# A decoder trunk on one core: three weight buffers made 64 bytes longer each, so that the operands behind them begin at other places of 512 bytes

## The chip, the cores and the metric

The kernel runs on one core of a Trainium2 chip. The metric is the device time of one execution in microseconds (us). All inputs and the output lie in the chip's main memory (HBM); the core works on a memory of 128 partitions (SBUF) and the matrix engine writes its sums to a small accumulator memory (PSUM).

## The reference

One layer of a decoder trunk on 2048 tokens of width 1024, in float32:

```python
mod = (c_act @ w_ada[l] + b_ada[l])[:, None, :]
sh1, sc1, g1, sh2, sc2, g2 = jnp.split(mod, 6, axis=-1)
h = rms_norm(x) * (1.0 + sc1) + sh1
x = x + g1 * token_mixer(h, w_in[l], ..., pos)
h = rms_norm(x) * (1.0 + sc2) + sh2
x = x + g2 * conv_ffn(h, w_up[l], conv_w[l], conv_b[l], w_down[l])
return rms_norm(x) * final_gain
```

`token_mixer` is one input projection, three groups of causal recurrent heads (retention, HGRN2, GLA) and one output projection. `conv_ffn` is an up-projection to 2 x 2816 columns, a causal convolution of width 3, a gated product and a down-projection.

## The kernel before

**Matrix products in halves.** Every large float32 product is made of three matmuls of the type float32r. Each operand is split into a high part (`hi`, the value rounded by a copy on ScalarE) and a low part (`lo`, the rest, by a subtraction on VectorE), and `split3` (L241 to L243) adds hi x hi, hi x lo and lo x hi into one accumulator. A matmul has one operand that is loaded into the matrix engine ahead of it (LDWEIGHTS, 128 columns; PEld in the profile) and one that is streamed through it (512 or 256 columns). The load of the next matmul runs beside the stream of the present one.

**The mixer** (four blocks of 512 tokens) takes about the first half of the time. `piece` (L217) and `tf512` (L281) fetch a piece of a weight matrix of 128 x 1024 values into a raw buffer and split it into `hi` and `lo`; `cf_gemm`, `tf_gemm` and `tf512` multiply the pieces with the normed input `h` (tile `ha`, both parts), `unit_g` multiplies `h` with a narrow weight of 32 columns (`alow`, L729 and L730), and `out_half` multiplies the mixer's outputs `oT` with `wout`. Between them lie the small float32 matmuls of the recurrences (`lvh`, `uh`, `ur` and others).

**The gated MLP** (two halves of 1024 tokens) follows. Up and down projections use a scheme with seven products in place of eight for a 2 x 2 block product; their operands are the tiles `A` and `dA` (weights, from `w4_tile`, L962) and `B` and `dB` (inputs, from `hc_tile`, L953).

**Order.** The order on the matrix engine is written out by hand (a clock in the program decides where the small matmuls go between the large ones); the other engines are ordered by a scheduler from the same program. All DMAs but 56 are issued from SP's queue.

**Where buffers lie.** Pools take room in the order in which they are opened: constants, `h`, `a4`, `w`, `tmp`, `x`, and then the mixer's `unit` and `const1`, whose room `gemm` takes over for the MLP. The pool `w` holds, in this order, two raw buffers (`wraw`), three high parts (`whi`) and three low parts (`wlo`), each 4096 bytes per partition. In the MLP the same eight buffers serve in turn as places for `A` and `dA`. All of this stands in the allocation of the built program, from which the following places are taken; "place" means the start address within a partition, modulo 512 bytes. Before the change every float32r operand begins at place 128, the slices of `alow` excepted, which are 128 bytes wide and begin at 128, 256, 384 and 0 in turn.

Of the kernel before, what the change touches and what calls it, by code (L numbers as in the profile page):

```python
# [10 lines left out]
F32R = mybir.dt.float32r  # L11
# [6 lines left out]
P = 128  # L18
# [36 lines left out]
class Clock:  # L55
# [15 lines left out]
    def adv(self, us):  # L71
        self.t += us
        while self.due and self.due[0][0] <= self.t:
            self._next()
# [26 lines left out]
def trunk(ctx, tc, xT, vecs, cvec, cst, rope, msk, wada, win, walow, wgla, wout, wup, wdown, out):  # L101
# [6 lines left out]
    pw = sb("w", 3)  # L108
# [9 lines left out]
    def acc_ps(name):  # L118
        return pp.tile([P, 512], F32, tag="acc", name=name, bufs=4)
# [17 lines left out]

    V, S, G, T = nc.vector, nc.scalar, nc.gpsimd, nc.tensor

    vec = pc.tile([P, 117], F32, tag="vec", name="vec")  # L140
    nc.sync.dma_start(vec[:], vecs[:, 0:117])
    c_all = pc.tile([P, NC_], F32, tag="cst", name="c_all")
# [62 lines left out]
    def keep(key, t):  # L205

        kept[key] = pdr.tile([P, 1024], F32, tag=f"kept{key}", name=f"kept{key}")
        nc.sync.dma_start(kept[key][:], t.bitcast(F32))
# [3 lines left out]
    def ada_next():  # L212
        m = later.pop(0) if later else None
        if m is not None:
            ada(m)

    def piece(src, name, key, both=False, ahead=50):  # L217

        ada_next()
        with tc.high_priority(offset=ahead):  # L220
            hi = pw.tile([P, 1024], F32R, tag="whi", name="h" + name)
            lo = pw.tile([P, 1024], F32R, tag="wlo", name="l" + name)
            if key + "h" in kept:
                nc.sync.dma_start(hi[:].bitcast(F32), kept[key + "h"][:])
                nc.sync.dma_start(lo[:].bitcast(F32), kept[key + "l"][:])
                return hi, lo
            raw = pw.tile([P, 1024], F32, tag="wraw", name="r" + name, bufs=NRAW)
            nc.sync.dma_start(raw[:], src)
            S.copy(hi[:], raw[:])
            if key + "l" in kept:  # L230
                nc.sync.dma_start(lo[:].bitcast(F32), kept[key + "l"][:])
            else:
                V.tensor_tensor(lo[:], raw[:], hi[:], op=ALU.subtract)  # L233
                if both:
                    keep(key + "h", hi[:])
                keep(key + "l", lo[:])
        return hi, lo

    def split3(ps, lhs, rhs, first, last, more=False):

        T.matmul(ps, lhs[0], rhs[0], start=first, stop=False, skip_group_check=more)  # L241
        T.matmul(ps, lhs[0], rhs[1], start=False, stop=False, skip_group_check=more)  # L242
        T.matmul(ps, lhs[1], rhs[0], start=False, stop=last, skip_group_check=more)  # L243

    h = [None] * KD
# [5 lines left out]
    def cf_gemm(name, i, parts=(slice(0, TB),)):  # L251
        if name in ready:
            return ready.pop(name)
        hi, lo = piece(win[i], name, f"i{i}")
        ps = acc_ps("ps" + name)
        for ts in parts:
            for k in range(KD):
                sl = slice(k * P, (k + 1) * P)
                split3(ps[:, ts], (hi[:, sl], lo[:, sl]), (h[k][:, 0, ts], h[k][:, 1, ts]), k == 0, k == KD - 1)
                adv(3 * M512)  # L260
        return ps
# [19 lines left out]
    def tf512(name, i):  # L281

        pss = [acc_ps(f"ps{name}_{c}") for c in range(NCH)]
        for q4 in range(4):
            half, sub = q4 // 2, q4 % 2
            src = win[i + half:i + half + 3:2][:, :, sub * 512:(sub + 1) * 512].rearrange("a p n -> p a n")
            ada_next()
            with tc.high_priority(offset=50):
                raw = pw.tile([P, 2, 512], F32, tag="wraw", name=f"r{name}_{q4}", bufs=NRAW)
                nc.sync.dma_start(raw[:], src)  # L290
                hi = pw.tile([P, 2, 512], F32R, tag="whi", name=f"h{name}_{q4}")
                lo = pw.tile([P, 2, 512], F32R, tag="wlo", name=f"l{name}_{q4}")
                S.copy(hi[:], raw[:])
                key = f"t{i}_{q4}l"
                flat = lo[:].rearrange("p a n -> p (a n)")
                if key in kept:
                    nc.sync.dma_start(flat.bitcast(F32), kept[key][:])
                else:
                    V.tensor_tensor(lo[:], raw[:], hi[:], op=ALU.subtract)
                    keep(key, flat)  # L300
            for c in range(NCH):
                cs = slice(c * P, (c + 1) * P)
                for kk in range(2):
                    k = half * 4 + sub * 2 + kk
                    sl = slice(kk * 256, (kk + 1) * 256)
                    split3(pss[c][:].rearrange("p (a n) -> p a n", a=2), (h[k][:, 0, cs], h[k][:, 1, cs]),
                           (hi[:, :, sl], lo[:, :, sl]), k == 0, k == KD - 1)
                    adv(3 * M512)
        return pss
# [60 lines left out]
    def startup():  # L370
# [8 lines left out]
        def weight(name, i, extra=False):  # L379
            raw = pw.tile([P, 1024], F32, tag="wraw", name="r" + name, bufs=NRAW)  # L380
            nc.sync.dma_start(raw[:], win[i])
            if extra:
                t = [pa.tile([P, 1024], F32R, tag="a4k", name=n + name) for n in "hl"]
            else:
                t = [pw.tile([P, 1024], F32R, tag="w" + n, name=n[0] + name) for n in ("hi", "lo")]
            W[name] = [*t, raw, i]

        def cast(name):
# [9 lines left out]
        def load(*ms):  # L398
            for m in ms:
                raws[m] = ada_load(m, True)  # L400
        load(8, 0)
        weight("f", 1)
        load(9)
        weight("q", 0)
        load(1, 2)
        acc = new_acc("n1_0")
# [47 lines left out]
        for k, (ld, first, then, wl) in enumerate(plan):  # L454
            if k == 0:
                weight("v0", 2)
            if k == 3:
                weight("v1", 3, True)
            load(*ld)
            for m in first:  # L460
                cond(m)
            scaled(x[k], bc[:], k)
            high(x[k], k, "0_")
            if k in (1, 4):
                name = "v0" if k == 1 else "v1"
                cast(name)
                parts[0].add(name)
            for m in then:
                cond(m)
            low(x[k], k)  # L470
            if wl:
                low_part(wl)
                parts[1].add(wl)
            pending += [(kind, k, w) for w in (0, 1) for kind in "fqv"]
            flush()
# [413 lines left out]
    def out_piece(b, half, i):  # L889
        return piece(wout[half * 4 + i], f"wo{b}_{half}_{i}", f"o{half * 4 + i}",  # L890
                     both=True, ahead=250 if (b, half) == (0, 0) else 600 if (b, half) == (NB - 1, 1) else 50)
# [57 lines left out]
    def take(ring, places):  # L949
        nth[ring] += 1  # L950
        return places[(nth[ring] - 1) % len(places)]
# [9 lines left out]

    def w4_tile(name):  # L962
        tag, bufs = take("w4", W4)
        return pw.tile([P, 1024], F32R, tag=tag, name=name, bufs=bufs)

    R_H, R_HC, R_A4 = [(ph, "h", 8, True)] * 8, [(None, "hc", 8, True)] * 8, [(pa, "a4k", NA4, True)] * NA4
# [20 lines left out]
    def up_op(A, s, f, i, src):  # L987
        t = w4_tile(f"A{s}_{f}_{i}")
        A[i] = split(src, t[:, 0:512], t[:, 512:1024])
# [307 lines left out]
    def last_operands(s):  # L1297

        r = []
        for k in range(NF // 2):  # L1300
            nm = f"{s}_3_{k}"
            with tc.high_priority(offset=60):
                ra = raw_half(sums["d", k][:, BLOCK[3], :], "rd" + nm)
                at = pa.tile([P, 1024], F32R, tag="a4k", name="dA" + nm) if k < 8 else w4_tile("dA" + nm)
                A = split(ra, at[:, 0:512], at[:, 512:1024])
                rb = t2k("rb" + nm)
                nc.sync.dma_start(rb[:], gs[s, 3, k][:])
                bt = ph.tile([P, 2, 512], F32R, tag="h", name="dB" + nm, bufs=8) if k < 8 else \
                    pg.tile([P, 2, 512], F32R, tag="hc", name="dB" + nm, bufs=8)
                r.append((A, split(rb[:], bt[:, 0, :], bt[:, 1, :])))  # L1310
        return r
# [233 lines left out]
def _build(arrays):  # L1545
    import concourse.bacc as bacc
    nc = bacc.Bacc("TRN2", target_bir_lowering=False, num_devices=1)
    aps = [nc.dram_tensor(n, a.shape, mybir.dt.from_np(a.dtype), kind="ExternalInput").ap()
           for n, a in arrays.items()]
    out = nc.dram_tensor("out", (NB, P, KD, TB), F32, kind="ExternalOutput").ap()  # L1550
    with tile.TileContext(nc) as tc:
        trunk(tc, *aps, out)
    return nc
# [10 lines left out]
```

## Time and profile before

| | us |
|---|---|
| median of three timed runs | 2562.22 |
| lowest and highest of them | 2557.1 and 2563.71 |
| span of the profiled execution | 2557.2 |
| PE (matmuls) busy in it | 2493.1 |
| PEld (weight loads) busy | 2132.7 |
| DVE busy | 1973.8 |
| ACT busy | 1139.0 |

The profiled execution is one of its own; the page gives its span from the first to the last instruction and no further time for it. The span lies at the low end of the three timed runs, 5.0 us (0.2%) under their median. PE is the matrix engine, DVE is VectorE, ACT is ScalarE. A matmul's end is modelled in the profile: a matmul of 512 columns is shown with 0.39 us, though the next one starts earlier. The pace is therefore read from the starts.

### The profile page before, as it was taken

What the parts mean: (1) busy time and instruction counts of PE and PEld (TensorE: products, weight loads), DVE (VectorE), ACT (ScalarE), POOL (GpSimd) and SP (SyncE); (2) the same over time, 40 slices, a digit from 0 to 9 for tenths busy, and PEclk for the clock granted to TensorE, in tenths of its full rate; (3) what the DMA queues carried; (4) which work ended last, traced back from release to release, by engine and by line L of the source; (5) the groups of instructions that cost most, each with busy time, mean ns of one, the idle gap of its engine ahead of it and who ended that gap; (6) DMA issues with size and microseconds to landing.
All of it is one profiled execution on the core that took longest, in us unless ns stands there. A gap on an engine that the chain in (4) does not pass through costs nothing.

```text
span 2557.2 us, 37116 instructions
## 1 busy us (share of the span) xinstructions
PE 2493.1 (97%) x13146; PEld 2132.7 (83%) x13146; DVE 1973.8 (77%) x3596; ACT 1139.0 (45%) x1914; POOL 169.6 (7%) x303
## 2 busy tenths in 40 slices
PE   5999999999999999999899999999999999999998
PEld 4898888988889898898788888888878888888887
DVE  8788986878678776787688888887677778778666
ACT  4433434524444235333254555455444555455442
POOL 1000000000000000000200000000001001000000
PEclk9999999999999999999999999999999999999999
DMA  8454576775687847786745444477675544447663
GB/s 304 166 190 165 197 250 214 250 251 196 220 309 278 291 147 242 267 308 223 278 168 174 153 146 163 149 274 244 210 228 168 155 146 145 154 136 251 221 193 127
DMA packets 229337, 533.84 MB, mean 209 GB/s; under 512 B 25216, under 2 KB 28320, under 8 KB 229152
## 3 DMA queue, kind: packets, MB, share of 16 engines
q1 hardware_dynamic: 224672, 516.80, 59.5%
q0 software_dynamic: 4480, 14.68, 1.6%
q8 instruction: 103, 1.69, 0.3%
q14 instruction: 82, 0.67, 0.1%
HBM read 397.69 MB, written 133.69 MB: 208 GB/s over the span
## 4 chain that ended last, share of the span: by engine, by line
PE 78%; issue 9%; DVE 5%; DMA 4%; ACT 1%; SPq 0%; POOL 0%; DVEq 0%; ACTq 0%; POOLq 0%
PE X L241 6%; PE X L242 6%; PE X L243 6%; PE Z L241 3%; PE Z L242 3%; PE Z L243 3%; PE lvh L610 3%; PE y L241 2%; PE y L243 2%; PE y L242 2%; PE psqkvgr L243 2%; PE psqkvgr L241 2%; PE psqkvgr L242 2%; PE psvgh L242 2%; PE psvgh L241 2%
## 5 line engine op out<-in xcount | busy, mean ns | idle before, releaser
L241 PE MATMUL X<-B,A 128*128 128x512 f32 x572 | 223.5, 391 | 1.4 <-ACT u L1247 1.4
L242 PE MATMUL X<-B,A 128*128 128x512 f32 x572 | 222.9, 390 | 0.0
L243 PE MATMUL X<-B,A 128*128 128x512 f32 x572 | 222.9, 390 | 0.0
L974 DVE TENSOR_TENSOR dA<-rd,dA 128x512 fp32r<-128x512 f32 x154 | 106.1, 690 | 86.7 <-ACT dA L973 86.4
L973 ACT CAST dA<-rd 128x512 fp32r<-128x512 f32 x154 | 95.6, 621 | 139.9 <-PE dX L243 45.8
L974 DVE TENSOR_TENSOR A<-s,A 128x512 fp32r<-128x512 f32 x176 | 120.8, 686 | 43.7 <-ACT A L973 43.3
L973 ACT CAST A<-s 128x512 fp32r<-128x512 f32 x176 | 108.7, 618 | 71.5 <-PE Z L243 45.2
L241 PE MATMUL psvgh<-hvgh,ha 128*128 128x256 f32 x480 | 140.0, 292 | 0.0
L241 PE MATMUL dX<-dB,dA 128*128 128x512 f32 x352 | 137.1, 390 | 0.0
L243 PE MATMUL dX<-dB,dA 128*128 128x512 f32 x352 | 137.1, 390 | 0.0
L242 PE MATMUL dX<-dB,dA 128*128 128x512 f32 x352 | 137.1, 390 | 0.0
L242 PE MATMUL psvgh<-lvgh,ha 128*128 128x256 f32 x480 | 135.9, 283 | 1.1 <-DVE lvgh L233 1.1
L243 PE MATMUL psvgh<-hvgh,ha 128*128 128x256 f32 x480 | 135.9, 283 | 0.0
L241 PEld LDWEIGHTS X<-B,A 128*128 128x128 f32 x572 | 107.5, 188 | 24.3 <-ACT u L1247 2.2
L243 PEld LDWEIGHTS X<-B,A 128*128 128x128 f32 x572 | 107.5, 188 | 22.1
L242 PEld LDWEIGHTS X<-B,A 128*128 128x128 f32 x572 | 107.5, 188 | 22.1
L610 PEld LDWEIGHTS lvh<-qbh,kh 128*128 128x128 f32 x896 | 115.2, 191 | 8.8 <-issue 1.0
L610 PE MATMUL lvh<-qbh,kh 128*128 128x128 f32 x896 | 120.1, 277 | 1.1 <-DVE kh L620 1.0
L241 PE MATMUL Z<-B,A 128*128 128x512 f32 x308 | 120.6, 392 | 0.0
L242 PE MATMUL Z<-B,A 128*128 128x512 f32 x308 | 120.5, 391 | 0.0
L243 PE MATMUL Z<-B,A 128*128 128x512 f32 x308 | 120.4, 391 | 0.0
L974 DVE TENSOR_TENSOR dB<-rb,dB 128x512 fp32r<-128x512 f32 x154 | 105.7, 687 | 13.2 <-ACT dB L973 13.1
(463 smaller groups left out, 7129.8 us busy)
## 6 DMA issues: line engine op xcount, KB each, us to landing
gs<-yv SPq DMA_DIRECT2D x154, 256.0 KB, 2.8
rb<-gs SPq DMA_DIRECT2D x154, 256.0 KB, 4.0
r<-wup SPq DMA_DIRECT2D x141, 256.0 KB, 3.3
s<-sumsu SPq DMA_DIRECT2D x132, 256.0 KB, 3.0
wada<-wada SPq DMA_DIRECT2D x48, 512.0 KB, 5.1
rd<-sumsd SPq DMA_DIRECT2D x88, 256.0 KB, 3.8
rd<-wdown SPq DMA_DIRECT2D x66, 256.0 KB, 3.8
x<-xT SPq DMA_DIRECT2D x64, 256.0 KB, 5.6
```

Of the source, the lines that this page charges most:

```text
L241: T.matmul(ps, lhs[0], rhs[0], start=first, stop=False, skip_group_check=more)
L242: T.matmul(ps, lhs[0], rhs[1], start=False, stop=False, skip_group_check=more)
L243: T.matmul(ps, lhs[1], rhs[0], start=False, stop=last, skip_group_check=more)
L610: T.matmul(ps[:, c * P:(c + 1) * P].rearrange("p (h n s) -> p h n s", h=2, s=s), kq[:, c * P:(c + 1) * P], rhs, start=True, stop=True)
L973: S.copy(hi, src)
L974: V.tensor_tensor(lo, src, hi, op=ALU.subtract)
```

## The change

Each `whi` buffer is allocated with 1040 columns of 4 bytes in place of 1024, and the first 1024 are used. The four places that made such a tile now call one helper.

```diff
+    def high_part(name):
+
+        return pw.tile([P, 1024 + 16], F32R, tag="whi", name=name)[:, 0:1024]
+
@@ piece
-            hi = pw.tile([P, 1024], F32R, tag="whi", name="h" + name)
+            hi = high_part("h" + name)
@@ tf512
-                hi = pw.tile([P, 2, 512], F32R, tag="whi", name=f"h{name}_{q4}")
+                hi = high_part(f"h{name}_{q4}").rearrange("p (a n) -> p a n", a=2)
@@ weight (startup)
-                t = [pw.tile([P, 1024], F32R, tag="w" + n, name=n[0] + name) for n in ("hi", "lo")]
+                t = [high_part("h" + name), pw.tile([P, 1024], F32R, tag="wlo", name="l" + name)]
@@ w4_tile
+        if tag == "whi":
+            return high_part(name)
```

In the built program this moves the second `whi` buffer by 64 bytes, the third by 128, and everything that lies behind them (`wlo`, and the pools `tmp`, `x`, `unit`, `const1`, `gemm`) by 192. Constants, `h`, `a4`, the raw buffers and the first `whi` buffer stay.

| place of 512 | before | after |
|---|---|---|
| `h`, `a4`, `wraw`, first `whi` | 128 | 128 |
| second, third `whi` | 128 | 192, 256 |
| `wlo`, `te`, `xy`, `hc`, most of `unit` | 128 | 320 |
| `kT`, `o`, `kk` (small float32 matmuls) | 320 | 0 |

## The prediction

> **What bounds the kernel now.** I read the page's totals first, then four stretches of the MLP.
>
> ```profile
> span 2557.2 us, 37116 instructions
> PE 2493.1 (97%) x13146; PEld 2132.7 (83%) x13146; DVE 1973.8 (77%) x3596; ACT 1139.0 (45%) x1914; POOL 169.6 (7%) x303
> ...
> 1400.00:1500.00 100.00, 100.00 (x443) 82.85 (x442) 83.31 (x106) 49.30 (x74) 7.01 (x20) 1.00 0.48 156
> 1700.00:1800.00 100.00, 100.00 (x443) 82.88 (x442) 69.94 (x110) 51.08 (x89) 0.00 (x0) 1.00 0.80 269
> 2000.00:2100.00 100.00, 100.00 (x443) 82.92 (x442) 78.28 (x97) 50.33 (x75) 9.54 (x11) 1.00 0.50 154
> 2200.00:2300.00 100.00, 100.00 (x443) 82.91 (x442) 77.60 (x95) 51.29 (x74) 9.35 (x10) 1.00 0.44 140
> ```
>
> PE is shown busy for 97% of the span. That alone says little, since a matmul's end is modelled. The stretches say more: their columns are the stretch, its length, busy time and count of PE, PEld, DVE, ACT and POOL, the granted clock, the DMA share and GB/s. In each 100 us exactly 443 matmuls are under way, at full clock, whether DMA is 0.44 or 0.80 busy and whether DVE is at 70 or at 83 us. So nothing but PE's own pace sets the time there. The timeline gives the pace; the first two rows are the first and the last of 28 matmuls of 512 columns that follow each other without a gap, the other two the first and the last of 15 of 256 columns:
>
> ```profile
> 1999.76 0.39 PE L242 MATMUL X<-B,A 128*128 128x512 f32 x1
> ...
> 2005.88 0.39 PE L242 MATMUL X<-B,A 128*128 128x512 f32 x1
> ```
> ```profile
> 517.18 0.28 PE L243 MATMUL psvgh<-hvgh,ha 128*128 128x256 f32 x1
> ...
> 518.85 0.28 PE L242 MATMUL psvgh<-lvgh,ha 128*128 128x256 f32 x1
> ```
>
> That is (2005.88 - 1999.76) / 27 = 226.7 ns for 512 columns and (518.85 - 517.18) / 14 = 119.3 ns for 256. The difference, 107.4 ns, is what 256 columns cost, so 512 columns cost 214.8 ns, and about **11.9 ns of each matmul do not depend on its width**. By the built program there are 8,422 float32r matmuls of 512 columns and 1,668 of 256: 8,422 x 0.2267 + 1,668 x 0.1193 = 2,108 us of the span. In these, the 11.9 ns amount to 10,090 x 0.0119 = 120 us. This is the only large sum on which the place of an operand could act.
>
> **The change, part by part.** The two built programs have the same 22,589 instructions in the same order on every engine, with the same waits; only addresses differ (and the row length of 1040 in the operands that lie in `whi`). So nothing is added, removed or moved in time by itself, and no queue sees another order. What remains are four possible prices.
>
> *1. PE reads with the two operands at other places.* A weight load runs beside the stream of the matmul before it. Before, the load and the stream beside it begin at the same place of 512 bytes in all cases but the 48 loads of `alow` at its other three places. After, by the built program, they begin at different places in 5,669 of the 8,422 and 1,184 of the 1,667 cases: about 6,850. What a different place costs or saves isn't shown for a full load. The nearest rows are those of `alow`, a narrower load with the same stream: its slices begin at 128, 256, 384 and 0 in turn, while the stream always begins at 128. Each place is used by two matmuls (L729, L730):
>
> ```profile
> 375.13 0.39 PE L729 MATMUL alg<-ha,alow 128*32 128x512 f32 x1
> 375.36 0.40 PE L730 MATMUL alg<-ha,alow 128*32 128x512 f32 x1
> 375.59 0.40 PE L729 MATMUL alg<-ha,alow 128*32 128x512 f32 x1
> 375.83 0.39 PE L730 MATMUL alg<-ha,alow 128*32 128x512 f32 x1
> 376.06 0.40 PE L729 MATMUL alg<-ha,alow 128*32 128x512 f32 x1
> 376.29 0.39 PE L730 MATMUL alg<-ha,alow 128*32 128x512 f32 x1
> 376.52 0.40 PE L729 MATMUL alg<-ha,alow 128*32 128x512 f32 x1
> 376.75 0.40 PE L730 MATMUL alg<-ha,alow 128*32 128x512 f32 x1
> 376.99 0.40 PE L241 MATMUL psakg<-ha,hakg 128*128 128x512 f32 x1
> ```
>
> The pair at the same place as the stream takes 375.59 - 375.13 = 0.46 us, the pairs that are 128, 256 and 384 bytes off take 0.47, 0.46 and 0.47. So none of the three other places saves the fixed 11.9 ns per matmul, and none adds it. The resolution: three pairs at other places take 376.99 - 375.59 = 1.40 us, 0.467 each, against 0.46; that is at most 3.3 ns per matmul. The second row of evidence is the small float32 matmuls, from the chain of work, eight of 128 columns in each group:
>
> ```profile
> 203.19 0.89 PE lvh L610 x8
> ...
> 211.10 0.89 PE uh L646 x8
> ...
> 297.63 0.89 PE ur L816 x8
> ```
>
> `lvh` reads both operands at place 128; `uh` and `ur` load `kT` and `kk` from 320 and stream `v` from 128. All take 0.89 us. They stream at a slower pace (0.89 / 8 = 111 ns for 128 columns), so they are the weaker evidence.
>
> There is also a reason from the rows why a start place should matter little:
>
> ```profile
> L729 PEld LDWEIGHTS alg<-ha,alow x32: 107/108/113, 59.1 to 983.5; 128*32 128x32 f32 x32
> ...
> L241 PEld LDWEIGHTS X<-B,A 128*128 128x128 f32 x572 | 107.5, 188 | 24.3 <-ACT u L1247 2.2
> ```
>
> A load of 32 columns is shown with 108 ns (the middle of the three figures), one of 128 with 188 (the mean), so a loaded column takes (188 - 108) / 96 = 0.83 ns, and a streamed one 107.4 / 256 = 0.42 ns. While the load goes through its 512 bytes, the stream goes through 1,024: their distance changes by 512 bytes and takes every value modulo 512 once, wherever they began. The start place moves that meeting, it doesn't take it away. I take **0** for this part, and keep 6,850 x 3.3 ns = 23 us to both sides as its bound, below nothing too.
>
> *2. DVE and ACT with operands at other places.* DVE's subtractions and products of 512 columns already come with all sorts of distances:
>
> ```profile
> L974 DVE TENSOR_TENSOR A<-s,A 128x512 fp32r<-128x512 f32 x176 | 120.8, 686 | 43.7 <-ACT A L973 43.3
> L700 DVE TENSOR_TENSOR qkh<-sqh,kh 128x512 f32<-128x512 f32 x16 | 11.0, 688 | 0.1
> L546 DVE TENSOR_TENSOR oh<-oh,sgh 128x512 f32<-128x512 f32 x16 | 11.0, 690 | 0.1
> L973 ACT CAST A<-s 128x512 fp32r<-128x512 f32 x176 | 108.7, 618 | 71.5 <-PE Z L243 45.2 <-DMA s<-sumsu 18.6 <-DVE s L1173 7.6
> L973 ACT CAST dB<-rb 128x512 fp32r<-128x512 f32 x154 | 94.9, 617 | 20.4 <-DMA rb<-gs 19.0 <-PE X L243 0.5
> ```
>
> `s` lies at place 224 and `A` at 128; `sqh`, `kh` and `qkh` all lie at 128; `oh` lies at 320 and `sgh` at 128. They take 686, 688 and 690 ns. ACT's casts take 618 and 617 ns, both from 224 to 128. I take 0. What covers a small loss is PE: of 100 us, DVE is busy 70 to 83 and ACT about 50.
>
> *3. DMA into and out of rows that begin elsewhere.* Every tile behind `whi` is moved by 192 bytes. How much DMA can matter is bounded by where PE waits for it, and by the start, the one stretch in which PE stands idle for long:
>
> ```profile
> PE y L243 <- DMA lwo<-kepto7l: 1.6, 1, 1.6
> PE y L241 <- DMA hwo<-kepto7h: 0.8, 1, 0.8
> ...
> 0.00:60.00 60.00, 33.09 (x164) 26.78 (x165) 47.94 (x83) 23.32 (x34) 12.06 (x24) 1.00 0.82 304
> ```
>
> PE's waits put down to DMA are 1.6 + 0.8 = 2.4 us in all; at the start 60 - 33.1 = 26.9 us are idle, in part for loads. If every load became 5% slower or faster (a guess, no row shows such a change), that would be 0.05 x (2.4 + 26.9) = 1.5 us. I take 0. The Trainium skill (DMA: Bandwidth & Descriptors, How a descriptor splits into AXI transactions) says that a row that doesn't begin at a multiple of 256 bytes costs extra beats; a row of 2,048 bytes would go from 68 beats at place 128 to 66 at place 320, an estimate of 3% less, which would make 0.9 us of those 29.3. No run here shows it.
>
> *4. Room.* The 192 bytes more change no pool's number of buffers, so no wait is made.
>
> The sum is 0 + 0 + 0 + 0, so a profiled execution would again span 2557.2 us. The median of the three runs stands 5.0 us above that, and the forecast is for such a median: **2562.2 us**.
>
> **The rivals.** *A: the 11.9 ns are a collision of the load with the stream beside it, and other places remove it.* It speaks for it that the amount is the same for 512 and 256 columns, as it would be if each load took something from the stream once, and that before the change every full load begins at the stream's place. Against it speak the `alow` pairs and the sweep. If it goes in all 6,850 cases, 6,850 x 0.0119 = 82 us go and the time is **2481 us**; at the bound of the `alow` rows it is 23 us, 2539. The Trainium skill (TensorE: Matmul & The Clock Gate, Part 1, "Wait — 56ns, not 53.3ns?") gives 215.7 ns between the starts of back-to-back matmuls of 512 columns, where the trace has 226.7; by it something does hold these up by 11 ns. Its figure is for bf16 matmuls, so it doesn't say what.
>
> *B: the same place is the good case, and other places cost.* When load and stream begin at the same place, they meet only at the ends of the load; from different places the stream overtakes the load in its middle. If that holds the stream up for two to three loaded columns (2.5 ns at 0.83 each), 6,850 x 2.5 ns = 17 us are added: **2579 us**; the bound above gives 2585. For it speaks that the `alow` pairs at other places are, if anything, the slower ones (0.467 against 0.46); against it that 0.01 us is one step of the view. It decides from 7.7 us / 6,850 = 1.1 ns per case on, since about 0.3% or 7.7 us is what a measurement here can tell from no change.
>
> *C: DMA sets something after all*, in the start or at the change from mixer to MLP, by up to 2 us to either side: 2560 to 2564. It can't be told from the forecast.
>
> That the change doesn't do what it says is excluded: the built program has the operands of the large matmuls at 128, 192, 256 and 320, and those of the small ones at 0 besides.
>
> **How the numbers follow.** The forecast has 0.62, A 0.18, B 0.16, C 0.04. C is within 0.3% for the most part; 0.01 of it goes to each side. So faster by over 0.3% gets 0.18 + 0.01 = 0.19, slower 0.16 + 0.01 = 0.17, and the rest, 0.64, is within 0.3%. The range takes in the bound of part 1 to both sides, 2562.2 - 23 and 2562.2 + 23: 2539 to 2585. It leaves out the full form of A and a little of B, some 0.14.
>
> **What would show it.** In the profile after: again 443 matmuls in each 100 us of the MLP, 27 steps of float32r matmuls in 6.12 us, `alow` pairs of 0.46 to 0.47 us though `alow` has moved to place 320, and DVE and ACT at 686 to 690 and 617 to 618 ns. A is right if the steps of matmuls with different places fall toward 215 ns while those with equal places (an `A` in the first `whi` with its `B` in an `h` tile) stay at 226.7. B is right if they rise by more than 1 ns. Equal steps and another time would mean that the waits at the start or between the stages have changed, and that part 3 is wrong.

## The result, and the profile after

The changed kernel takes 2584.3 us (median of 4 runs, 2581.43 to 2588.4) against 2562.97 us before (4 runs). The ratio is **1.0096, 95% interval 1.0084 to 1.0109**: about 24.6 us slower. That is 0.0096 of the time before, and the table below is in such microseconds; the two medians by themselves lie 21.3 us apart. The profiled execution took 2581.43 us, with a span of 2579.7, 22.5 us more than the span before. The forecast was no change, with a range of 2539 to 2585.

The totals of the page after, and the same four stretches of the MLP (stretch, length, then busy time and count of PE, PEld, DVE, ACT and POOL, granted clock, DMA share, GB/s):

```profile
span 2579.7 us, 37116 instructions
PE 2516.3 (98%) x13146; PEld 2128.2 (83%) x13146; DVE 1974.9 (77%) x3596; ACT 1136.1 (44%) x1914; POOL 170.1 (7%) x303
```
```profile
1400.00:1500.00 100.00, 100.00 (x437) 81.74 (x437) 83.53 (x106) 49.59 (x74) 7.70 (x22) 1.00 0.45 151
1700.00:1800.00 100.00, 100.00 (x436) 81.50 (x435) 72.94 (x111) 52.62 (x91) 0.00 (x0) 1.00 0.81 274
2000.00:2100.00 100.00, 100.00 (x435) 81.28 (x434) 75.91 (x92) 48.70 (x72) 9.37 (x10) 1.00 0.49 153
2200.00:2300.00 100.00, 100.00 (x435) 81.42 (x434) 78.20 (x96) 48.77 (x74) 9.48 (x11) 1.00 0.45 145
```

PE is still never idle there and the clock is still full, but only 435 to 437 matmuls are under way in 100 us in place of 443. That is 1.66%; on the 1,267 us from 1290 to the end it would make 21 of the 22.5 us. The starts of the first matmul of the up-projection and of the last `dX` of the down-projection, before and after, bear it out:

```profile
1227.36 0.58 PE L241 MATMUL X<-B,A 128*128 128x512 f32 x1
...
2510.28 0.39 PE L243 MATMUL dX<-dB,dA 128*128 128x512 f32 x1
```
```profile
1228.33 0.58 PE L245 MATMUL X<-B,A 128*128 128x512 f32 x1
...
2532.48 0.40 PE L247 MATMUL dX<-dB,dA 128*128 128x512 f32 x1
```

The MLP begins 1.0 us later and, up to that last `dX`, takes 22.2 - 1.0 = 21.2 us more. PE's busy time has grown by 23.2 us, and those of DVE, ACT and POOL have changed by 3 us at most. In the lines of the groups (busy us, mean ns of one), DVE and ACT take what they took; PE's waits for DMA sum to 2.2 us in place of 2.4; and the float32 matmuls, now with `kT` at place 0 and `vh` at 320, still take 0.89 us for eight:

```profile
L980 DVE TENSOR_TENSOR A<-s,A 128x512 fp32r<-128x512 f32 x176 | 120.7, 686 | 48.5 <-ACT A L979 48.1
L704 DVE TENSOR_TENSOR qkh<-sqh,kh 128x512 f32<-128x512 f32 x16 | 11.0, 686 | 0.1
L550 DVE TENSOR_TENSOR oh<-oh,sgh 128x512 f32<-128x512 f32 x16 | 11.0, 689 | 0.1
L979 ACT CAST dB<-rb 128x512 fp32r<-128x512 f32 x154 | 95.0, 617 | 20.2 <-DMA rb<-gs 18.8 <-PE X L247 0.5
```
```profile
PE y L247 <- DMA lwo<-kepto7l: 1.6, 1, 1.6
PE y L245 <- DMA hwo<-kepto7h: 0.6, 1, 0.6
```
```profile
240.69 0.89 PE lvh L614 x8
...
251.89 0.89 PE uh L650 x8
```

So what has changed is the pace of the float32r matmuls. The changed kernel has its own control, since its operands lie at several places. The timeline, put beside the built program's addresses, has long stretches in which load and stream keep one distance modulo 512 (place of the loaded operand less that of the streamed one beside it). First and last matmul of three of them:

```profile
2422.15 0.39 PE L245 MATMUL dX<-dB,dA 128*128 128x512 f32 x1
...
2430.10 0.39 PE L247 MATMUL dX<-dB,dA 128*128 128x512 f32 x1
```
```profile
1321.81 0.40 PE L245 MATMUL X<-B,A 128*128 128x512 f32 x1
...
1329.60 0.39 PE L246 MATMUL Z<-B,A 128*128 128x512 f32 x1
```
```profile
1751.50 0.40 PE L245 MATMUL dY<-dB,dA 128*128 128x512 f32 x1
...
1759.67 0.39 PE L247 MATMUL dX<-dB,dA 128*128 128x512 f32 x1
```

The first has distance 0 (both at 320): 7.95 us / 35 steps = 227.1 ns. The second has distance 192 (128 streamed, 320 loaded): 7.79 / 34 = 229.1. The third has 320 (320 streamed, 128 loaded): 8.17 / 35 = **233.4**. The same kernel, the same engines beside it, three paces. The single steps repeat: in the second stretch they run 226, 229, 232 ns over and over, in the third they alternate between 231 and 236.

### The profile page after: what moved, and what is told of

It is laid out like the page before. It is cut to its first block, busy times and chain, and to the rows that moved or that the text cites. A ratio compares the mean times of both kernels' runs of the same rounds, so it can differ in the third digit from the quotient of the medians.

```text
span 2579.7 us, 37116 instructions
## 1 busy us (share of the span) xinstructions
PE 2516.3 (98%) x13146; PEld 2128.2 (83%) x13146; DVE 1974.9 (77%) x3596; ACT 1136.1 (44%) x1914; POOL 170.1 (7%) x303
## 4 chain that ended last, share of the span: by engine, by line
PE 81%; issue 9%; DVE 4%; DMA 3%; ACT 1%; POOL 0%; SPq 0%; DVEq 0%; ACTq 0%; POOLq 0%
PE X L245 6%; PE X L247 6%; PE X L246 6%; PE lvh L614 3%; PE Z L245 3%; PE Z L247 3%; PE Z L246 3%; PE psvgh L246 2%; PE psvgh L245 2%; PE psvgh L247 2%; PE psqkvgr L246 2%; PE psqkvgr L245 2%; PE psqkvgr L247 2%; PE lvg L614 2%; PE y L245 2%
## 5 line engine op out<-in xcount | busy, mean ns | idle before, releaser
L980 DVE TENSOR_TENSOR A<-r,A 128x512 fp32r<-128x512 f32 x130 | 89.2, 687 | 33.0 <-ACT A L979 33.0
```

The source lines that it names most:

```text
L980: V.tensor_tensor(lo, src, hi, op=ALU.subtract)
```

## The experiments

The theory to be tested: only the distance between a load and the stream beside it sets the pace. Rivals: the place of each operand by itself (multiples of 128 bytes being good), the other engines' or DMA's work at moved rows, or which of the moved buffers are in it.

**Matmuls alone, a map of the distance.** Nothing of the trunk is computed; 48 matmuls in a row for each pair of places.

```python
def r32(o, q, n, cols=P):
    return lambda r: (st[:, o + (r % 8) * P:o + (r % 8) * P + cols],
                      mv[:, q + (r % 4) * 512:q + (r % 4) * 512 + n])
...
for o in range(0, 128, 4):
    run("S", 4 * o, r32(o, 0, 512), 512)
```

> This kernel leaves out the whole computation and runs matmuls alone, 48 in a row for each pair of places, with nothing beside them: S moves the loaded operand by 0 to 496 bytes in steps of 16, M the streamed one, B both, H is S with 256 columns, N with 32 loaded columns, F in float32, L is bf16, T has the third load of each three moved. Theory one (only the distance between load and stream modulo 512 counts): S at 0 and all of B at 226 to 228 ns per matmul; S at 64, 128, 320 and 384 at 231 to 234 and at 192 and 448 at 229 to 231, as in the changed kernel's MLP; M mirrors S (distance -d); H falls by 1 to 2 ns at 320 and 448; N and F stay flat within 2 ns. Rival one (the place of each operand by itself counts, 128-byte multiples being good): B rises at 64, 192, 320 and 448 and stays at 0, 128, 256, 384, and S is flat at 128, 256 and 384. Rival two (the places matter only beside other engines' work): all of S, M and B are flat at 226 to 228.

In the timeline each group of 48 is one row: start, length, name, count. The three letters behind the capital are the bytes, a for 0 to j for 9 (`Sage` is 064). A step is the difference of two starts divided by 48.

```profile
22.27 11.04 PE L55 MATMUL Saaa<-mv,st 128*128 128x512 f32 x48
33.15 11.05 PE L55 MATMUL Sabg<-mv,st 128*128 128x512 f32 x48
...
66.42 11.36 PE L55 MATMUL Sage<-mv,st 128*128 128x512 f32 x48
77.62 11.29 PE L55 MATMUL Saia<-mv,st 128*128 128x512 f32 x48
...
155.81 11.15 PE L55 MATMUL Sbjc<-mv,st 128*128 128x512 f32 x48
166.80 11.36 PE L55 MATMUL Scai<-mv,st 128*128 128x512 f32 x48
...
200.09 11.04 PE L55 MATMUL Scfg<-mv,st 128*128 128x512 f32 x48
210.97 11.05 PE L55 MATMUL Schc<-mv,st 128*128 128x512 f32 x48
...
477.32 11.08 PE L55 MATMUL Bage<-mv,st 128*128 128x512 f32 x48
488.24 11.08 PE L55 MATMUL Bbci<-mv,st 128*128 128x512 f32 x48
...
655.81 11.28 PE L55 MATMUL Nage<-mv,st 128*32 128x512 f32 x48
666.93 11.23 PE L55 MATMUL Nbci<-mv,st 128*32 128x512 f32 x48
...
744.27 10.88 PE L55 MATMUL Fage<-mf,sf 128*128 128x128 f32 x96
754.99 10.88 PE L55 MATMUL Fbci<-mf,sf 128*128 128x128 f32 x96
...
819.31 10.52 PE L55 MATMUL Laaa<-mh,sh 128*128 128x512 bf16 x47
829.48 11.28 PE L55 MATMUL Taaa<-mv,st 128*128 128x512 f32 x48
840.60 11.25 PE L55 MATMUL Tage<-mv,st 128*128 128x512 f32 x48
851.69 11.28 PE L55 MATMUL Tbci<-mv,st 128*128 128x512 f32 x48
...
873.89 11.04 PE L55 MATMUL Tcfg<-mv,st 128*128 128x512 f32 x48
884.77 11.25 PE L55 MATMUL Tdca<-mv,st 128*128 128x512 f32 x48
```

- Distance 0: (33.15 - 22.27) / 48 = 226.7 ns. 64: 11.20 / 48 = 233.3. 192: 10.99 / 48 = 229.0. **256: 10.88 / 48 = 226.7**, as good as 0. The whole curve from 256 to 496 repeats that from 0 to 240 within 0.2 ns, one step of the rows. So the distance counts modulo 256, not 512 as the theory had it; the theory's other numbers hold.
- Both operands moved together (B, 64 bytes): 10.92 / 48 = 227.5, nearly all of it in the first few matmuls. The place by itself doesn't count: rival one falls. Nothing ran beside these matmuls, and the paces differ all the same: rival two falls.
- 32 loaded columns (N, 64): 11.12 / 48 = 231.7, the same at all distances within 1.1 ns. float32 (F): 10.72 / 96 = 111.7 at all distances. Neither kind feels it.
- The streamed operand moved (M) mirrors S: 64 bytes give 229.2, 192 give 233.3. With only each third load 64 bytes off (T): 11.09 / 48 = 231.0, well over a third of the way from 226.7, which T has at 256 bytes (10.88 / 48). T's row at 0 looks slower only because the first start in it is recorded too early, 417 ns before the second; its later steps take 226.7. So the matmuls at the good distance are slowed too when others come between them.
- Streams of 256 columns (H) take 120 ns at 0, 160 and 256 bytes, among the slowest, and are 1 to 3 ns faster at most other distances.
- bf16 with a load for each matmul, at distance 0: its row can't be divided as it stands, since one of the 48 matmuls is missing in it and the next row's first start is early. Two starts inside it, 36 matmuls apart, are 820.82 and 828.59: 7.77 / 36 = 215.8. The Trainium skill (TensorE: Matmul & The Clock Gate, Part 1, "Wait — 56ns, not 53.3ns?") gives 215.7 for bf16, and this agrees. So the further 11 ns come with float32r, and no distance in these runs takes them away under 512 columns.

**All operands moved alike.**

```diff
-    vec = pc.tile([P, 117], F32, tag="vec", name="vec")
+    vec = pc.tile([P, 117 + 48], F32, tag="vec", name="vec")[:, 0:117]
```

> The kernel before with its first constant tile 192 bytes longer, so that every later buffer begins 192 bytes further on: all large operands at place 320, none at another place than its partner. Theory one (only the distance between load and stream modulo 512 counts): the time of before, ratio 0.998 to 1.002, 443 matmuls in 100 us of the MLP. Rival one (a place that is no multiple of 128 costs by itself): at least as slow as the changed kernel, ratio 1.008 to 1.03, since all operands now begin at such a place. A rival on DMA or on the other engines (rows moved by 192 bytes cost there): most of the changed kernel's 1.0096, with 443 matmuls in 100 us.

Ratio 1.0002, interval 0.9991 to 1.0013 (2562.02 us). Again 443 in each stretch:

```profile
1400.00:1500.00 100.00, 100.00 (x443) 82.80 (x442) 83.33 (x106) 49.90 (x74) 7.03 (x20) 1.00 0.48 155
1700.00:1800.00 100.00, 100.00 (x443) 82.81 (x442) 71.30 (x111) 51.89 (x90) 0.00 (x0) 1.00 0.82 271
```

Everything behind `whi` begins where it does in the changed kernel, and no loss shows; the interval leaves room for 3.3 us at most. So DMA rows and the other engines at place 320 are not what costs 24.6 us.

**Four arrangements of the same buffers.** The steps of the map, one for each of the pairs of load and stream in the built program, give a sum for any arrangement. (Pairs with `alow` are left out, and small float32 matmuls in between are passed over.) For the changed kernel, worked out after its result, it is 28.3 us more for 512 columns and 2.3 less for 256: 26.0 us. The four kernels change `high_part` and put a gap behind the high parts; for the gap of 256 bytes:

```diff
+    padded = []
+
     def high_part(name):
 
-        return pw.tile([P, 1024 + 16], F32R, tag="whi", name=name)[:, 0:1024]
+        t = pw.tile([P, 1024 + 0], F32R, tag="whi", name=name)
+        if not padded:
+            padded.append(pw.tile([P, 64], F32, tag="gap", name="gap", bufs=1))
+        return t[:, 0:1024]
```

The others: 32 columns of gap (128 bytes); 1040 columns for `whi` and a gap of 16 columns; 1024 for `whi` and a gap of 48 columns.

> The changed kernel with all three high parts 4096 bytes again, and one gap of 256 bytes between the high and the low parts: everything behind lies at place 384, everything else at 128, so half of the operands are 256 bytes off their partner modulo 512. Theory one, as the run with matmuls alone mended it (the distance counts modulo 256): the time of before, ratio 0.998 to 1.002. Rival (the distance counts modulo 512, any other than 0 costs): 1.007 to 1.010.

> As the run with the gap of 256 bytes, with a gap of 128: everything behind the high parts lies at place 256, all else at 128. Theory one: 3,861 pairs of 512 columns are 128 bytes off, modulo 256, at 6.8 ns each, and 512 pairs of 256 columns gain 1.2 ns each: 26.3 - 0.6 = 25.6 us more, ratio 1.010 (1.007 to 1.012). Rival (starts at multiples of 128 bytes are good, 64 and 192 are what costs): the time of before, 0.998 to 1.002.

> The change with a gap of 64 bytes behind the third high part: the second and third high parts stay at places 192 and 256, everything behind them comes to 384, which is 128 modulo 256. So only two of the eight weight buffers are off. Theory one, with the nanoseconds of the run with matmuls alone for each pair: 16.6 us more for 512 columns, 1.2 us less for 256, together 15.4 us, ratio 1.006 (1.004 to 1.008). Rival (the cost sits in what lies behind, DMA rows and low parts included): 1.000 to 1.002.

> The other part alone: the high parts are 4096 bytes again and stay at place 128, and a gap of 192 bytes behind them brings everything else to 320, as in the changed kernel. Theory one, by the same sum: 19.6 us more for 512 columns, 1.1 us less for 256, together 18.4 us, ratio 1.007 (1.005 to 1.009). Rival (the cost sits in the two high parts at 192 and 256): 1.000 to 1.002.

| kernel | sum by the map | ratio measured (95%) | in us |
|---|---|---|---|
| the change | 26.0 us | 1.0096 (1.0084 to 1.0109) | 24.6 |
| all moved alike | 0 | 1.0002 (0.9991 to 1.0013) | 0.5 |
| gap of 256 | 0 | 1.0004 (0.9996 to 1.0013) | 1.0 |
| gap of 128 | 25.6 us | 1.0098 (1.0085 to 1.0111) | 25.1 |
| two high parts alone | 15.4 us | 1.0059 (1.0046 to 1.0071) | 15.1 |
| what lies behind alone | 18.4 us | 1.0079 (1.0066 to 1.0092) | 20.2 |

All these rivals fall. 256 bytes off costs nothing that shows, so the period holds in the kernel too. 128 off costs as much as the whole change though every operand begins at a multiple of 128. Each part of the change alone costs, and together they cost less than their sum: 24.6 against 35.3, and by the map 26.0 against 33.8, since a pair whose two operands both move is off in each part but counts once in the change (2,638 and 3,858 pairs of 512 columns are off in the parts, 5,606 in the change). Rows of 1040 columns aren't needed for the loss either: the gap of 128 and "what lies behind alone" have rows of 1024. Rows of 1040 with all places equal were not run.

The totals agree better than their parts. By the map, the MLP's pairs of the changed kernel cost about 17 us and the mixer's about 9; in the profiled executions the MLP took 21.2 us more and the mixer 1.0. Put beside the addresses, the starts in the MLP show one reason: its 2,084 steps at distance 0 take 228.4 ns in the mean, where the kernel before has 226.7. That is 3.5 us that the map puts at nothing. In the mixer, PE's idle time between 60 and 1230 us falls from 11.2 to 8.8 us, which takes up a part of the loss; the rest isn't explained. So the agreement of the totals is in part luck.

One row of each of two kernels in the stretch from 1400, first of the gap of 256, then of 128:

```profile
1400.00:1500.00 100.00, 100.00 (x443) 82.81 (x442) 83.20 (x106) 49.98 (x74) 7.04 (x20) 1.00 0.49 155
```
```profile
1400.00:1500.00 100.00, 100.00 (x437) 81.71 (x436) 84.37 (x106) 49.12 (x74) 7.12 (x21) 1.00 0.46 148
```

**Finer steps: is some distance better than 0?**

> Matmuls alone again, the computation left out, 48 for each pair of places: S moves the loaded operand in steps of 4 bytes from 0 to 252 under streams of 512 columns, H in steps of 16 under 256 columns, J and K load 64 and 96 columns in place of 128, Q and R stream 384 and 128 columns. Theory one (load and stream meet at a part of the memory that is picked by the address modulo 256, and the best distance is already had at 0): no S under 226 ns, steps of 226.7 for distances of up to about 16 bytes to either side of 0 and 229 to 234 elsewhere; H between 117 and 120; J and K between the flat 231.6 of 32 columns and the curve of 128. Rival (some distance frees the stream of the fixed 11.9 ns): one or more S at 214 to 222 ns.

No group with 128 loaded and 512 streamed columns is under 226.6 ns, so the rival falls. Matmuls with 64 and 96 loaded columns vary with the distance too (228 to 233 ns, and not always between 32 and 128 columns), streams of 384 columns vary from 173 to 177, and streams of 128 columns not at all (111.6 ns at 64, 128 and 192). But the theory's smooth hollow around 0 isn't there either: 4 bytes off gives 232.5, and 16 bytes, 226.7 in the first map, gives 233.4 here, while 144 bytes has gone from 233.3 to 226.9. The row of 140 bytes, that of 144 and the one behind them:

```profile
412.00 11.36 PE L55 MATMUL Sbea<-mv,st 128*128 128x512 f32 x48
423.20 11.05 PE L55 MATMUL Sbee<-mv,st 128*128 128x512 f32 x48
434.09 11.37 PE L55 MATMUL Sbei<-mv,st 128*128 128x512 f32 x48
```

140 bytes: 11.20 / 48 = 233.3; 144: 10.89 / 48 = 226.9. A third run asked whether what ran before decides.

> Matmuls alone, the computation left out. Each distance (0, 16, 64, 128, 144, 192 and 240 bytes; 0, 64, 128 and 192 under streams of 256 columns) is run 48 times right after 48 matmuls of another distance: C and H after distance 0, D and I after 64, E and J after 128, G and K after 192. In the two earlier runs distances 16 and 144 gave 226.7 in one and 233.3 in the other. Theory one, mended (the pace is a beat between load and stream that keeps the phase with which it was entered): 0 gives 226.7 after any, while 16, 144 and 240 give 226.7 or 230.0 or 233.3 depending on what ran before. Rival (the distance alone sets the pace, and the two earlier runs differ by something else): each distance gives one pace within 0.3 ns whatever ran before.

```profile
55.44 11.04 PE L55 MATMUL Cabg<-mv,st 128*128 128x512 f32 x48
66.32 11.04 PE L55 MATMUL PCage<-mv,st 128*128 128x512 f32 x48
...
209.17 11.36 PE L55 MATMUL Dabg<-mv,st 128*128 128x512 f32 x48
220.37 11.36 PE L55 MATMUL PDage<-mv,st 128*128 128x512 f32 x48
...
669.67 5.82 PE L55 MATMUL Hage<-mv,st 128*128 128x256 f32 x48
675.33 11.08 PE L55 MATMUL PHbci<-mv,st 128*128 128x512 f32 x48
...
736.72 5.61 PE L55 MATMUL Iage<-mv,st 128*128 128x256 f32 x48
742.17 11.35 PE L55 MATMUL PIbci<-mv,st 128*128 128x512 f32 x48
```

It does. 16 bytes after distance 0: 10.88 / 48 = 226.7; after distance 64: 11.20 / 48 = 233.3. Under 256 columns, 64 bytes after distance 0: 5.66 / 48 = 117.9; after 64: 5.45 / 48 = 113.5. Distance 0 comes to 226.7 within some ten matmuls after each of the others, and 64 gives 233.3 each time. Of the seven distances under 512 columns, the other five have more than one pace: 144 has 226.7 and 233.3, 240 has 226.7 and 228.4, 192 has about 229 and 233, 128 lies between 232.4 and 233.2. The rival (the distance alone) falls. The mended theory holds in the main, load and stream falling into a repeating pattern that what ran before helps to choose; the paces that it named for 240 after other distances (230.0 or 233.3) were missed, and so was the second pace at 192 bytes.

## Why the prediction was wrong

**The step that failed is part 1**, "I take 0 for this part": a full load (128 columns) that begins at another place, modulo 256, than the stream beside it does cost time, 24.6 us / 6,850 = 3.6 ns for each case in the mean, and 6.6 ns where 64 bytes lie between them in the map. The time of 2584.3 us lies 0.7 us inside the stated range, but that is luck: the range's bound of 3.3 ns was the resolution of rows that don't feel the effect. Two things stood behind the 0.

- *The nearest row was of a kind that doesn't feel the effect.* The `alow` pairs were flat, were read rightly, and are flat after the change too, at 0.46 to 0.47 us. But the map shows that a load of 32 columns is nearly flat over the distances, while one of 128 columns isn't: 226.7 to 234.2 in steps of 16 bytes. A narrower load was taken for a small version of the full one. The rows had a hint of it: `alow`'s matmuls took 230 to 235 ns each, more than the 226.7 of those with a full load at the same place. The float32 rows were flat for the same reason: float32 doesn't feel it. The only rows about full loads were those behind the fixed 11.9 ns, and they had equal places throughout, so none of the rows shown could give the price.
- *The sweep was no argument.* That load and stream pass every distance once wherever they begin was taken to mean that the start doesn't matter. The runs show that the start, together with what ran before, decides the pattern that they fall into: 226.7 at 0, 233.3 at 64.

Part 2 (other engines) and part 3 (DMA) were right: the rows of DVE, ACT and the waits for DMA are unchanged, and moving all rows by 192 bytes costs 0.5 us, which can't be told from nothing. The 0.9 us that the Trainium skill (DMA: Bandwidth & Descriptors, How a descriptor splits into AXI transactions) would let one expect, by the prediction's estimate, is too small for these runs to show.

The rivals: **B was what happened**, same place good and other places bad, and its point of decision (1.1 ns per case) was passed; but it had 0.16, and its price of 17 us was too low. The 5,606 pairs with 128 loaded and 512 streamed columns that came to lie off cost 28.3 us by the map, 5.1 ns each in the mean, while by the map the pairs of 256 columns gave 2.3 us back. B's mechanism, that the stream overtakes the load in its middle, is not shown, only its sign. A was wrong for 512 columns, where no distance in any run is under 226.6 ns, and half right for 256, which it put with the others: there distance 0 is one of the slow ones, 120.0 ns against 113.3 to 117.8 at 64 and 192 bytes. (By the map the fixed part at distance 0 is 2 x 120.0 - 226.7 = 13.3 ns, and about half of it goes at 113.3.) C didn't matter.

The count of cases was right. It counted modulo 512 where 256 is the period, but that makes no difference here: the large operands lie at 128, 192, 256 and 320, the slices of `alow` 128 bytes apart from 320 on, and none lies 256 bytes from the stream beside it.

A version that keeps distance 0 for the streams of 512 columns and has another for those of 256 might be faster than the kernel before; it wasn't tried. None of the kernels run is shown to be faster than the kernel before.

## What to carry to other kernels

Where TensorE is the bound and float32r operands lie in buffers whose lengths are multiples of 256 bytes, keep them so: here 64 bytes more in three buffers cost 1%, and no wait in the trace showed it. Pad by 256 bytes or not at all, or move everything together. Before a flat row is taken as evidence, ask whether its shape (columns loaded, type) could show the effect; here the cheap test was matmuls alone, 48 for each distance, and its table gave the price of four kernels in advance within 2 us, though for the change itself the split between mixer and MLP came out otherwise.

## What the runs showed of the hardware that was not expected

- The pace of float32r matmuls with 128 loaded and 512 streamed columns depends on the distance of the two operands' start addresses modulo 256 bytes: 226.7 ns at 0, 226.7 to 237 elsewhere, most often 233.3. The Trainium skill (TensorE: Matmul & The Clock Gate, Part 2, "Step-by-step: what each phase is for") says "Loading the next tile's weights doesn't steal SBUF read bandwidth from the running matmul." For bf16 the 215.8 ns at distance 0 don't contradict it. For float32r the distance costs up to 10 ns, so there the measurement decides against reading the sentence as "the load costs the stream nothing"; whether it is read bandwidth that is lost isn't shown.
- The pace isn't a function of the distance alone: the same 16 bytes ran at 226.7 or 233.3 by what ran before. And equal places don't shield a pair: after pairs at other distances, distance 0 takes some ten matmuls to come back to 226.7.
- With 256 streamed columns distance 0 takes 120.0 ns, 128 bytes 118.5 to 120.2, and 64 and 192 give 113.3 to 117.8, again by what ran before.
- Which part of the memory or of the engine the two meet in stays open: the runs vary addresses alone. They don't show either whether bf16 has such a map, since it was run at distance 0 only.
